# A decoder trunk's prologue: small tables loaded as rows, tile 0's gain behind its transposes, the first weight unit in halves, fillers on TensorE

## The chip, the cores and the metric

The kernel runs on one core of a Trainium2 chip. The metric is the device time of one execution in microseconds, the median of several. A core has TensorE (PE: matmuls, and PEld: its weight loads), VectorE (DVE), ScalarE (ACT), GpSimd (POOL) and SyncE (SP, which here only issues DMAs); each works off its own queue strictly in order, and they meet through semaphores. Sixteen DMA engines move data for all queues. The granted clock is the share of TensorE's full speed that the chip's throttle allowed.

## The reference

Two layers of a decoder trunk act on x of 512 tokens by 1024 features. Each layer normalizes x by its root mean square and a gain g (`norm_g`), projects it with one matrix to 3488 columns, feeds four head groups with these (latent attention, a short convolution, a spatial gate, block-sparse attention), multiplies each by a SiLU gate, projects back and adds the result to x.

```
def rmsnorm(x, g):
    xf = x.astype(jnp.float32)
    y = xf * lax.rsqrt(jnp.mean(xf * xf, axis=-1, keepdims=True) + EPS)
    return (y * g).astype(x.dtype)
...
    h = rmsnorm(x, norm_g)
    p = h @ w_in
...
    ang = pos.astype(jnp.float32)[..., None] * inv
    cos = jnp.cos(ang)[:, :, None, :]
    sin = jnp.sin(ang)[:, :, None, :]
```

The change touches only the way into the first layer: the loads of `positions`, g and the first weights, the normalization of x and the first projection. What is computed stays the same.

## The kernel before, in words

**Precision.** Every product is made of three matmuls (`mm3`, line 250). Both operands are split into a high part, which the reduced format fp32r holds, and a low part, the difference; hi by hi, hi by lo and lo by hi are summed in PSUM. So each weight and each activation is split once: ACT (sometimes DVE) copies it to the high part, and DVE subtracts (`split2`, line 245, and `split_units`, line 331).

**Tiles.** The 512 tokens are four tiles of 128. For each tile `pre_norm` (line 544) takes the sum of squares (ACT, two halves), lets GpSimd add the two and raise to the power -1/2 (two small steps on `xss`), multiplies x by that scale and by g on DVE to h, transposes h by eight 128x128 PE transposes in two groups of four (`hT`), and splits the result into `hTh` and `hTl`.

**Weights.** They arrive in units of at most 128x1024 elements, loaded in a fixed order by SP's queue (`load_units`, line 316). The first four, c0 to c3, hold the 416 columns of the first projection (`cq`): 256 contraction rows each, that is two of the eight k-steps. So k-steps 0 and 1 need c0, 2 and 3 c1, and so on. For every token tile, `tok` (line 1169) runs eight k-steps of three matmuls 128x416, 24 in all. A unit is split in two halves; a half is one k-step.

**Order.** A planner in Python (`Order` and `Chain`, lines 63 to 189) writes the program. Each piece of work is a generator, with a clock for each engine and a modelled cost for each operation; the planner emits an operation when its inputs are due by the model, smaller priorities first. What it emits is then the fixed order of each engine's queue. `o.now` is the modelled time of TensorE. A DMA is modelled at 360 bytes per ns plus 2 us. `LOAD_HOOKS` starts the loads of x tiles after given weight units. If the model is wrong, the order stays, and engines wait.

**The prologue** (`start`, line 1275). DVE sets a tile of ones and a zeroed tile `gz`; PE warms up with three matmuls of ones. SP loads x tile 0 in two halves, then g into the first row of `gz`, then c0, x tile 1, c1, c2, c3, x tiles 2 and 3. PE spreads g over 128 partitions by multiplying `gz` with the ones (`ng`, two PSUM tiles, kept until the last tile's h). GpSimd's queue loads the positions as a 128x4 tile of single elements (line 395); GpSimd and DVE later make the rope tables from it (`rope_tables`, line 400, from modelled time 7000 ns, with the lowest priority, in the gaps).

**After it.** Tile by tile: `cq`, its low-rank chain (`ct`, transposes `cT`, `q`, `kv`), then the unit sequence sq, ga, kv, su and so on, with the attention heads in between, then the output projection `o`, whose operands for block-sparse attention are called `yD`. Layer 1 follows in the same way.

## Time and profile before

| | before |
|---|---|
| median of 3 executions | 508.97 us (508.83 to 509.05) |
| profiled execution, its own time | 508.65 us |
| its span, first to last instruction | 506.8 us |
| PE busy | 498.1 us |
| mean granted clock of TensorE | 0.996 |
| first matmul of the first projection | 11.08 us |
| first weight unit c0: issued, in use from | 2.65, 7.78 us |
| positions: issued, in use from | 2.21, 7.30 us |

Times in the profile count from the start of the span. A row of the timeline gives start, duration, engine, source line, operation, output and inputs, shape and count; in brackets stand the time that the engine had been idle before and what ended it. All operations that the planner emits have line 158 (PE's: 184), so rows are told apart by their tiles: `whi_c` and `wlo_c` are the high and low part of a c unit, `sq` the squares, `xss` the scale, `h` the normalized tile, `hT` its transpose. Matmul durations overlap, since matmuls are pipelined; the step from one start to the next is their price.

### The profile page before, as it was taken

The page shows a single profiled execution, that of the slowest core. Times are in us where ns is not written, and L with a number is a line of the kernel's source. Part 1 is how long each engine was busy: PE and PEld are TensorE (multiplying, and loading weights), DVE is VectorE, ACT ScalarE, POOL GpSimd, SP SyncE. Part 2 cuts the span into 40 slices and gives each one's busy share as a digit, 9 for nine tenths or more (in the row PEclk, how much of TensorE's full clock was granted, in tenths as well). Part 3 has the DMA queues.
Part 4 walks back from the last instruction along what each step waited for, and adds up shares of the span by engine and source line. Part 5 has one row for each costly group of instructions (what it writes and reads, how often), then busy time and mean ns, then how long its engine had stood idle before and what let it go on. Part 6 is the DMA issues. An engine that isn't in the chain of part 4 may idle for free.

```text
span 506.8 us, 7665 instructions
## 1 busy us (share of the span) xinstructions
PE 498.1 (98%) x2508; PEld 423.3 (84%) x2508; DVE 349.3 (69%) x917; ACT 296.5 (58%) x891; POOL 139.2 (27%) x321
## 2 busy tenths in 40 slices
PE   6999999999999999999999999999999999999997
PEld 4898888888888888888889988888888888888886
DVE  4877975468799887635576988777868887635311
ACT  5698764567687775424247894677766777432100
POOL 6867875452000000000121488513330000000000
PEclk9999999999999999999999999999999999999999
DMA  8533415112114123464443242140142121624111
GB/s 273 165 123 114 125 43 166 41 43 66 60 43 166 52 74 109 142 175 117 143 155 126 83 125 71 55 124 2 42 167 82 43 83 49 201 84 164 66 54 50
DMA packets 20618, 51.57 MB, mean 102 GB/s; under 512 B 5985, under 2 KB 7265, under 8 KB 20578
## 3 DMA queue, kind: packets, MB, share of 16 engines
q1 hardware_dynamic: 20546, 51.08, 31.1%
q8 instruction: 20, 0.33, 0.3%
q0 software_dynamic: 32, 0.00, 0.1%
q14 instruction: 20, 0.16, 0.1%
HBM read 46.87 MB, written 4.19 MB: 101 GB/s over the span
## 4 chain that ended last, share of the span: by engine, by line
PE 90%; POOL 4%; DVE 2%; DMA 2%; ACT 1%; issue 1%; POOLq 0%; DVEq 0%
PE o L184 17%; PE kv L184 10%; PE cq L184 6%; PE sq L184 5%; PE cc L184 4%; PE gb L184 4%; PE cb L184 4%; PE gd L184 4%; PE gc L184 4%; PE ch L184 4%; PE su L184 4%; PE sa L184 3%; PE ga L184 3%; PE oa L184 2%; PE od L184 2%; PE sd L184 2%
## 5 line engine op out<-in xcount | busy, mean ns | idle before, releaser
L158 DVE TENSOR_TENSOR xr<-o,xr 128x512 f32<-128x512 f32 (+1 forms) x17 | 11.2, 658 | 42.0 <-PE o L184 42.0
L184 PE MATMUL o<-whi_wo,yTl 128*128 128x512 f32 (+1 forms) x102 | 38.4, 377 | 0.0
L184 PE MATMUL o<-wlo_wo,yTh 128*128 128x512 f32 (+1 forms) x102 | 38.4, 377 | 0.0
L184 PE MATMUL o<-whi_wo,yTh 128*128 128x512 f32 (+1 forms) x102 | 38.4, 376 | 0.0
L158 ACT ACTIVATE whi_wo<-raw_wo 128x512 fp32r<-128x512 f32 x31 | 18.3, 624 | 21.7 <-PE o L184 13.6
L158 ACT ACTIVATE pa<-pa,mna 128x256 f32<-128x256 f32 (+3 forms) x44 | 23.4, 539 | 5.2 <-DVE mna L158 5.1
L184 PE MATMUL kv<-whi_kv,hTh 128*128 128x512 f32 x64 | 26.0, 406 | 0.0
L184 PE MATMUL o<-whi_wo,yD 128*128 128x512 f32 (+1 forms) x68 | 25.7, 381 | 0.0
L158 ACT ACTIVATE pd<-pd,mnd 128x256 f32<-128x256 f32 (+3 forms) x46 | 24.5, 546 | 2.0 <-DVE mnd L158 1.5
L158 ACT ACTIVATE pha<-pTa 128x512 fp32r<-128x512 f32 (+3 forms) x32 | 13.9, 434 | 20.1 <-PE pTa L184 19.9
L184 PE MATMUL kv<-whi_kv,hTl 128*128 128x512 f32 x64 | 25.1, 392 | 0.0
L184 PE MATMUL kv<-wlo_kv,hTh 128*128 128x512 f32 x64 | 24.9, 390 | 0.0
L158 ACT ACTIVATE phd<-pTd 128x512 fp32r<-128x512 f32 (+3 forms) x32 | 13.9, 435 | 18.4 <-PE pTd L184 18.3
L184 PE MATMUL cq<-whi_c,hTh 128*128 128x416 f32 x64 | 24.3, 380 | 0.0
L184 PE MATMUL cq<-whi_c,hTl 128*128 128x416 f32 x64 | 23.3, 365 | 0.0
L184 PE MATMUL cq<-wlo_c,hTh 128*128 128x416 f32 x64 | 23.0, 360 | 0.0
L158 DVE TENSOR_TENSOR wlo_wo<-raw_wo,whi_wo 128x512 fp32r<-128x512 f32 x32 | 21.0, 687 | 2.4 <-ACT whi_wo L158 2.0
L184 PEld LDWEIGHTS o<-wlo_wo,yTh 128*128 128x128 f32 x102 | 19.2, 188 | 3.6
L184 PEld LDWEIGHTS o<-whi_wo,yTh 128*128 128x128 f32 x102 | 19.2, 188 | 3.6
L184 PEld LDWEIGHTS o<-whi_wo,yTl 128*128 128x128 f32 x102 | 19.2, 188 | 3.5
L158 DVE CUSTOM_DVE_ANT_0 pa<-sa,maskb 128x512 f32<-128x512 f32 (+3 forms) x32 | 15.0, 485 | 8.7 <-PE pTa L184 4.6
L158 DVE TENSOR_TENSOR pld<-pTd,phd 128x512 fp32r<-128x512 f32 (+3 forms) x32 | 15.5, 486 | 4.9 <-ACT phd L158 4.8
(328 smaller groups left out, 1712.8 us busy)
## 6 DMA issues: line engine op xcount, KB each, us to landing
raw_wo<-in_w_o_dram SPq DMA_DIRECT2D x16, 512.0 KB, 3.9
raw_sq<-in_w_t_dram SPq DMA_DIRECT2D x8, 512.0 KB, 3.5
raw_kv<-in_w_t_dram SPq DMA_DIRECT2D x8, 512.0 KB, 3.5
raw_c<-in_w_c_dram SPq DMA_DIRECT2D x8, 416.0 KB, 4.2
raw_ga<-in_w_f_dram SPq DMA_DIRECT2D x4, 512.0 KB, 3.6
raw_su<-in_w_f_dram SPq DMA_DIRECT2D x4, 512.0 KB, 3.5
raw_gc<-in_w_f_dram SPq DMA_DIRECT2D x4, 512.0 KB, 3.6
raw_ch<-in_w_f_dram SPq DMA_DIRECT2D x4, 512.0 KB, 3.4
```

What stands on the lines that cost most here:

```text
L158: f(*a, **k)
L184: f(*a, **k)
```

## The change

- The positions come as four rows of 128 by ACT's queue into `junk`; GpSimd casts them, one PE transpose turns them into a 128x4 tile, DVE copies it out (`posf`). g comes as eight rows of 128 by ACT's queue, and a PE transpose and a DVE copy make `gT`, 128x8, the gain of each feature by partition. The `gz` tile, its memset, its load and the `ng` matmuls are gone.
- Tile 0's h is x times the scale alone. Its gain is applied behind the transposes: ACT's copy to the high part scales by `gT`, and DVE multiplies and subtracts in one operation for the low part, both in pieces of one k-step (128 columns) in place of four. A tile's `hT` now has one event for each k-step. Tiles 1 to 3 multiply by g as before, from a 128x1024 copy that is now loaded by SP's queue behind c3 (`load_norm_gain`, as in layer 1).
- c0 is loaded in two halves. ACT makes both high parts. Both low parts are made by GpSimd, behind tile 0's scale (`split_first`). GpSimd also makes the low part of c1's second half and of c2's first half (`POOLLO`). Token tile 0 waits for a unit's half in place of the whole unit.
- The squares of tile 0 and 1 are shared between DVE (its first 640 or 512 columns, in one reducing operation) and ACT (the rest). x tile 0 is loaded in parts of 640 and 384 columns, and x tile 1 behind c1 in place of c0.
- Warm-up: two matmuls of ones ahead of the two small transposes, three behind. Until the planner's time 16000 ns, wherever PE waits by the model, transposes of the identity are put into 60% of the gap (`FILL`).
- Later starts and priorities: rope tables from 14000 ns in place of 7000, the mixing chain from 21000 in place of 23000, layer 0's parameters due at 16500 in place of 17500.

The lines that the diff removes from `pre_norm` and from the squares in `start` are printed above and left out here.

```
@@ -32,9 +32,11 @@
...
 AHEAD = 4
-NWARM, NWARM2 = 3, 1
-ROPET, MIXT = 7000.0, 23000.0
+NWARM, NWARM2, X0CUT = 2, 3, (640, 512)
+ROPET, MIXT = 14000.0, 21000.0
...
+FILL, FILLEND = 0.6, 16000.0
+POOLLO = (('c1_0', 1), ('c2_0', 0))
...
@@ -179,7 +181,11 @@
...
                 yield self.t + PEMARGIN
+        if self.o.now < self.o.fill_until:
+            for _ in range(int((self.o.now - self.o.pe_end) * FILL / 110.0)):
+                self.o.fill()
...
+        self.o.pe_end = self.o.now
...
@@ -322,7 +329,15 @@
...
                 u.raw = yield from rawS.get(ch, u.name)
-            dma(ch, P * u.a * u.b * 4, u.raw[:, :u.a * u.b], u.src)
+            n = u.a * u.b
+            if u.name == "c0_0":
+                for i in range(2):
+                    ch = Chain(o)
+                    sl = slice(i * n // 2, (i + 1) * n // 2)
+                    dma(ch, P * n * 2, u.raw[:, sl], u.src[:, sl])
+                    o.set(u.landed[i], ch.t)
+            else:
+                dma(ch, P * n * 4, u.raw[:, :n], u.src)
...
@@ -331,9 +346,13 @@
     def split_units():
...
             ch = Chain(o)
-            yield from ch.wait(u.loaded)
+            if u.name != "c0_0":
+                yield from ch.wait(u.loaded)
...
             n = u.a * u.b
+            if u.name == "c0_0":
+                yield from split_first(u, ch)
+                continue
...
@@ -346,16 +365,35 @@
...
                     yield from c2.act(A.activation, hi, raw, AF.Copy)
-                yield from c2.dve(V.tensor_tensor, lo, raw, hi.bitcast(F32), op=ALU.subtract)
+                if (u.name, i) in POOLLO:
+                    yield from c2.pool(G.tensor_tensor, lo, raw, hi.bitcast(F32), op=ALU.subtract)
+                else:
+                    yield from c2.dve(V.tensor_tensor, lo, raw, hi.bitcast(F32), op=ALU.subtract)
+                o.set(u.half[i], c2.t)
...
-    def unit(ch, name):
+    def split_first(u, ch):
+        n = u.a * u.b // 2
+        parts = [(u.hi[:, i * n:(i + 1) * n], u.lo[:, i * n:(i + 1) * n], u.raw[:, i * n:(i + 1) * n])
+                 for i in range(2)]
+        for i, (hi, _, raw) in enumerate(parts):
+            yield from ch.wait(u.landed[i])
+            yield from ch.act(A.activation, hi, raw, AF.Copy)
+        yield from ch.wait(layers[0].r0_ev)
+        for i, (hi, lo, raw) in enumerate(parts):
+            yield from ch.pool(G.tensor_tensor, lo, raw, hi.bitcast(F32), op=ALU.subtract)
+            o.set(u.half[i], ch.t)
+        u.raw_slots.put(ch)
+        o.set(u.ready, ch.t)
+    def unit(ch, name, half=None):
...
             v.wanted = True
-        yield from ch.wait(u.ready)
+        yield from ch.wait(u.ready if half is None else u.half[half])
...
@@ -389,10 +428,10 @@
...
     junk = cst.tile([P, GW], F32, name="junk")
-    posi = cst.tile([P, NT], I32, name="posi")
...
     inv = cst.tile([P, 16], F32, name="inv")
-    nc.gpsimd.dma_start(posi, dram(positions, 0, [[1, P], [P, NT]]))
+    nc.scalar.dma_start(junk[0:NT, 0:P].bitcast(I32), dram(positions, 0, [[P, NT], [1, P]]))
+    G.tensor_copy(junk[0:NT, P:2 * P], junk[0:NT, 0:P].bitcast(I32))
...
@@ -542,37 +580,61 @@
...
     def pre_norm(L, t, xx, t0, release):
...
+        late = L.l == t == 0
+        def half(c, t1):
+            c2 = Chain(o, t1)
...
             hput(c2)
...
+            nk = 1 if late else 4
+            todo = []
+            for k in range(0, 4, nk):
+                kt = c * 4 + k
+                hi, lo = (z[:, kt:kt + nk, t * P:(t + 1) * P] for z in (hTh, hTl))
+                src = tp[:, k * P:(k + nk) * P].rearrange("p (k n) -> p k n", k=nk)
+                ca = Chain(o, c2.t)
+                yield from ca.act(A.activation, hi, src, AF.Copy, **(dict(scale=gT[:, kt:kt + 1]) if late else {}))
+                todo.append((ca.t, kt, hi, lo, src))
+            for ta, kt, hi, lo, src in todo:
+                cv = Chain(o, ta)
+                if late:
+                    yield from cv.dve(V.scalar_tensor_tensor, lo, in0=src, scalar=gT[:, kt:kt + 1],
+                                      in1=hi.bitcast(F32), op0=ALU.mult, op1=ALU.subtract)
+                else:
+                    yield from cv.dve(V.tensor_tensor, lo, src, hi.bitcast(F32), op=ALU.subtract)
+                for i in range(nk):
+                    o.set(L.hT[t][kt + i], cv.t)
+            if c == min(t, 1):
+                o.set(L.hi_ev[t], ca.t)
+            trS.put(cv)
+        ch = Chain(o, t0)
+        s1 = L.xss[t]
+        eps = 0.0 if L.l == 0 and t < 2 else EPS
+        yield from ch.pool(G.tensor_scalar, s1[:, 2:3], s1[:, 0:1], s1[:, 1:2], eps, op0=ALU.add, op1=ALU.add)
+        yield from pow_rstd(ch, s1[:, 3:4], s1[:, 2:3], 1)
+        if t == 0:
+            o.set(L.r0_ev, ch.t)
+        if not late:
+            yield from ch.wait(L.ng_ev)
+        h = yield from hS.get(ch, f"h{t}_{L.l}")
+        hput = shared(hS, 2)
...
+            sl = slice(c * 512, (c + 1) * 512)
+            if late:
+                yield from ch.dve_fast(V.tensor_scalar, h[:, sl], xx[:, sl], s1[:, 3:4], None, op0=ALU.mult)
+            else:
+                yield from ch.dve(V.scalar_tensor_tensor, h[:, sl], in0=xx[:, sl], scalar=s1[:, 3:4], in1=L.ng[c],
+                                  op0=ALU.mult, op1=ALU.mult)
+            o.spawn(half(c, ch.t), None, t - NT)
+        release(ch)
+        if t == NT - 1:
+            for _ in range(2):
+                t2S.put(ch)
...
     def rope(ch, x1, x2, cb, sb, nh, nd, name):
...
@@ -1169,10 +1231,10 @@
         def tok(L, n, width, t, dst, us):
...
             for k in range(KT):
-                if n == "c" and k % 4 == 0:
-                    yield from m.wait(L.hT[t][k // 4])
-                if t == 0 and k % 2 == 0:
-                    us.append((yield from unit(m, f"{n}{k // 2}_{L.l}")))
+                if n == "c":
+                    yield from m.wait(L.hT[t][k])
+                if t == 0:
+                    us[k // 2:] = [(yield from unit(m, f"{n}{k // 2}_{L.l}", k % 2))]
...
@@ -1273,24 +1335,34 @@
...
     def start():
+        o.clk["D"] = 800.0
...
         ones = (yield from zzS.get(cw, "ones"))
-        gz = yield from hS.get(cw, "gz")
+        gn = ones[0:KT, 256:384]
+        nc.scalar.dma_start(gn, dram(norm_g, 0, [[P, KT], [1, P]]))
...
-        yield from cw.dve_fast(V.memset, gz, 0.0)
...
-        for _ in range(NWARM):
-            PE.matmul(wp[:, 0:256], ones[:, 0:P], ones[:, 0:256], start=True, stop=True)
+        def warm(n):
+            for _ in range(n):
+                PE.matmul(wp[:, 0:256], ones[:, 0:P], ones[:, 0:256], start=True, stop=True)
+        warm(NWARM)
+        PE.transpose(wp[:, 256:256 + NT], junk[0:NT, P:2 * P], ident[0:NT, 0:NT])
+        V.tensor_copy(posf, wp[:, 256:256 + NT])
+        PE.transpose(wp[:, 384:384 + KT], gn, ident[0:KT, 0:KT])
+        V.tensor_copy(gT, wp[:, 384:384 + KT])
+        warm(NWARM2)
+        o.pe_end, o.fill_until = 6300.0, FILLEND
+        o.fill = lambda: PE.transpose(wp[:, 0:P], ident, ident)
+        zzS.put(Chain(o, 6000.0))
+        accS.put(Chain(o, FILLEND + 200.0))
...
-        L0.ng = []
-        for c in range(2):
-            L0.ng.append((yield from sS.get(cg, f"ng{c}")))
...
         L0.x[0] = x0
-        for c in range(2):
-            dma(cg, P * 2048, x0[:, c * 512:(c + 1) * 512], x[0, 0:P, c * 512:(c + 1) * 512])
-            o.set(L0.x0[c], cg.t)
-        nc.sync.dma_start(gz[0:1, :], dram(norm_g, 0, [[D, 1], [1, D]]))
+        for c, sl in enumerate((slice(0, X0CUT[0]), slice(X0CUT[0], D))):
+            cx = Chain(o)
+            dma(cx, P * 4 * (sl.stop - sl.start), x0[:, sl], x[0, 0:P, sl])
+            o.set(L0.x0[c], cx.t)
...
         def after(t):
             def f():
@@ -1298,10 +1370,10 @@
...
             units[n].wanted = True
-        LOAD_HOOKS["c0_0"] = (after(1),)
-        LOAD_HOOKS["c3_0"] = (after(2), after(3))
+        LOAD_HOOKS["c1_0"] = (after(1),)
+        LOAD_HOOKS["c3_0"] = (lambda: o.spawn(load_norm_gain(L0)), after(2), after(3))
...
-        L0.par_t = 17500.0
+        L0.par_t = 16500.0
...
@@ -1309,25 +1381,28 @@
...
             def pre(t):
                 ch = Chain(o)
...
+                sq = yield from sS.get(ch, f"sq{t}")
+                if t:
+                    yield from ch.wait(L0.hi_ev[min(t - 1, 1)])
+                if t < 2:
+                    xt, s1, cut = L0.x[t], L0.xss[t], X0CUT[t]
+                    yield from ch.wait(L0.x0[0] if t == 0 else L0.xr[t])
+                    jk = yield from hS.get(ch, f"sqj{t}")
+                    yield from ch.dve(V.tensor_tensor_reduce, out=jk[:, 0:cut], in0=xt[:, 0:cut], in1=xt[:, 0:cut],
+                                      scale=1.0 / D, scalar=EPS, op0=ALU.mult, op1=ALU.add, accum_out=s1[:, 0:1])
+                    hS.put(ch)
+                    t1 = ch.t
+                    ch = Chain(o, L0.x0[1].t if t == 0 else max(L0.hi_ev[0].t, L0.xr[t].t))
+                    yield from ch.act(A.activation, sq[:, 0:D - cut], xt[:, cut:D], AF.Square, scale=D ** -0.5,
+                                      accum_out=s1[:, 1:2])
+                    ch.t = max(ch.t, t1)
+                else:
+                    yield from ch.wait(L0.xr[t])
+                    for c in range(2):
+                        yield from square_half(ch, L0, t, c, sq, L0.x[t])
...
                 yield from pre_norm(L0, t, L0.x[t], ch.t, v4S.put)
...
+            o.spawn(pre(t), None, t - NT)
...
```

51 lines of the change are left out of this document (6 added, 45 removed).

## The prediction

> **What bounds the kernel now.** I read the page first: one engine fills the span.
>
> ```profile
> PE 498.1 (98%) x2508; PEld 423.3 (84%) x2508; DVE 349.3 (69%) x917; ACT 296.5 (58%) x891; POOL 139.2 (27%) x321
> ```
>
> TensorE is busy for 98%, so only its idle or slow stretches can be won. The windows view places them (length, busy us of PE, PEld, DVE, ACT, POOL, granted clock, DMA share, GB/s).
>
> ```profile
> 4.74:8.15 3.41, 2.22 (x6) 0.86 (x5) 0.37 (x1) 0.56 (x3) 1.63 (x5) 1.00 0.92 226
> 8.15:11.56 3.41, 1.55 (x10) 1.11 (x10) 3.38 (x8) 2.26 (x7) 3.05 (x7) 1.00 1.04 422
> 11.56:14.98 3.42, 3.42 (x11) 3.15 (x11) 2.94 (x6) 3.15 (x8) 3.01 (x6) 0.50 1.02 402
> 14.98:22.26 7.28, 6.68 (x42) 6.01 (x40) 5.56 (x11) 4.28 (x13) 6.16 (x14) 1.00 0.33 99
> 22.26:503.30 481.04, 480.99 (x2440) 409.96 (x2437) 335.43 (x892) 283.69 (x860) 122.32 (x266) 1.00 0.30 96
> ```
>
> From 22.26 to the last matmul PE is idle for 0.05 us. Ahead of it lie an idle start, 3.42 us at half the clock, and a few holes. The timeline of PE gives the steps:
>
> ```profile
> 10.67 0.66 PE L184 MATMUL hT<-ident,h 128*128 128x128 f32 x4 [0.50 <-DVE h L158]
> 11.08 0.43 PE L184 MATMUL cq<-whi_c,hTh 128*128 128x416 f32 x1
> 12.10 0.55 PE L184 MATMUL cq<-whi_c,hTh 128*128 128x416 f32 x1
> 14.87 0.41 PE L184 MATMUL cq<-whi_c,hTl 128*128 128x416 f32 x1
> 17.83 0.60 PE L184 MATMUL hT<-ident,h 128*128 128x128 f32 x4
> 18.18 0.43 PE L184 MATMUL cq<-whi_c,hTh 128*128 128x416 f32 x1
> 18.64 0.35 PE L184 MATMUL cq<-whi_c,hTl 128*128 128x416 f32 x1
> 20.34 0.35 PE L184 MATMUL cq<-whi_c,hTl 128*128 128x416 f32 x1
> 21.25 0.55 PE L184 MATMUL cT<-ident,ct 128*128 128x128 f32 x3 [0.55 <-DVE ct L158]
> 22.26 0.43 PE L184 MATMUL cq<-whi_c,hTh 128*128 128x416 f32 x1
> ```
>
> Nine steps lie between 18.64 and 20.34: a cq matmul costs 0.189 us. Eight lie between 12.10 and 14.87: 0.346 us at the low clock. Tile 0's 24 cq matmuls run from 11.08, and at 18.18 tile 1 begins, with tile 0 and both transpose groups of tile 1 done. I call that **state S**; the sum is the time at which the new kernel reaches S. A transpose group costs 0.35 us (17.83 to 18.18). From 18.18 to 22.26 stand 12 matmuls (2.27), one such group and three cT transposes (at most 0.35 each): 2.97 us in 4.08, so 1.1 us more is lost after S.
>
> Why so late a start? Four rows of DVE and ACT, then SyncE and GpSimd:
>
> ```profile
> 3.45 0.60 ACT L158 ACTIVATE sq<-x 128x512 f32<-128x512 f32 x1 [1.37 <-DMA x<-in_x_dram]
> 7.78 0.39 DVE L158 CAST whi_c<-raw_c 128x416 fp32r<-128x416 f32 x1 [5.50 <-DMA raw_c<-in_w_c_dram]
> 8.71 0.74 DVE L158 SCALAR_TENSOR_TENSOR h<-x,xss,ng 128x512 f32<-128x512 f32 x1
> 13.05 0.58 DVE L158 TENSOR_TENSOR wlo_c<-raw_c,whi_c 128x416 fp32r<-128x416 f32 x1
> ```
>
> ```profile
> 2.21 0.99 POOL L395 DMA_DIRECT2D posi<-in_positions_dram  x1
> 2.30 0.30 SPq L1293 DMA_DIRECT2D gz<-in_norm_g_dram  x1
> 2.65 0.35 SPq L259 DMA_DIRECT2D raw_c<-in_w_c_dram  x1
> 5.04 0.30 POOL L158 TENSOR_SCALAR xss<-xss 128x1 f32<-128x1 f32 x1 [1.21 <-ACT sq L158]
> 5.42 0.58 POOL L158 TENSOR_TENSOR xss<-xss,nhalf 128x1 f32<-128x1 f32 x1
> 7.30 0.19 POOL L158 CAST posf<-posi 128x4 f32<-128x4 int32 x1 [1.30 <-DMA posi<-in_positions_dram]
> 11.64 0.99 POOL L158 TENSOR_SCALAR xss<-xss 128x1 f32<-128x1 f32 x1
> 13.04 1.04 POOL L158 TENSOR_TENSOR xss<-xss,nhalf 128x1 f32<-128x1 f32 x1
> ```
>
> Tile 0's scale is ready at 5.42 + 0.58 = 6.00, but DVE is stuck in its queue behind the first weight half, which lands at 7.78; h starts at 8.71. That load was issued at 2.65, behind gz. The DMA view from 5 to 6 us shows what held it:
>
> ```profile
> DMA packets 50, 0.08 MB, mean 82 GB/s; under 512 B 27, under 2 KB 27, under 8 KB 50
> ## 3 DMA queue, kind: packets, MB, share of 16 engines
> q1 hardware_dynamic: 33, 0.08, 68.4%
> q0 software_dynamic: 17, 0.00, 50.9%
> ```
>
> Queue q0 is the positions, element by element: half of the 16 engines' time for no bytes, 82 GB/s against 422 later.
>
> **The change part by part.** *Positions and g as rows.* 6 KB in two issues on ACT, 0.35 us each by SyncE's row at 2.65, before its first square at 3.45: hidden. The chain that they head is new: GpSimd waits for the positions before its cast (behind it 0.6 us of memsets and tile 0's scale), PE for cast and rows (behind it the warm-ups and the transposes), DVE for PE (behind it tile 0's square). The slow q0 packets go, and gz with its memset and its place before c0; so c0's two halves are issued at about 1.7 and 2.1 and land at about 4.7 and 5.3 (estimate: the 0.52 MB of x ahead of them, then 0.43 MB at 422 GB/s is 1.0 us). What is late next is not c0.
>
> *Tile 0's squares.* DVE's two-operand reduction, at two widths:
>
> ```profile
> L158 DVE CUSTOM_DVE_ANT_0 pa<-sa,maskb 128x512 f32<-128x512 f32 x8 | 5.5, 686 | 3.1 <-PE sa L184 3.0
> L158 DVE CUSTOM_DVE_ANT_0 pa<-sa,maskb 128x384 f32<-128x384 f32 x8 | 4.4, 554 | 1.6 <-PE pTa L184 1.6
> ```
>
> 640 columns: 0.686 + 0.132 = 0.82 us, from about 4.1 (x at 3.45 plus the wider part; the two small copies of posf and gT stand ahead of it on DVE and wait for PE, which waits for the rows). It ends near 5.0, where GpSimd began before (5.04). So the scale is again ready at 6.0; I book nothing. h follows at once, PE transposes at 6.5, the eight hi and eight lo pieces follow one by one (128 columns are 0.29 us by the same step, so four pieces cost DVE 0.5 us more than one of 512; beside PE's wait below), and the first cq matmul starts near 7.8 instead of 11.08. This early start is not the sum: weights come next.
>
> *Low parts on GpSimd.* Both halves of c0, c1's second and c2's first go to GpSimd, in a queue that begins when the scale is ready (6.0), and by the planner's own costs tile 1's two scale steps stand ahead of the fourth. k-steps 4 to 7 of tile 0 cannot start before that fourth part. The trace has no GpSimd subtraction 416 wide; its nearest rows:
>
> ```profile
> L158 POOL TENSOR_TENSOR mq<-mq,cosT x14: 244/252/285, 93.6 to 327.8; 128x32 f32<-128x32 f32 x14
> L158 POOL TENSOR_TENSOR Q<-Q,cosT x6: 313/320/862, 73.0 to 92.1; 128x64 f32<-128x64 f32 x6
> ```
>
> 32 more columns cost 0.068 us, so 416 cost 0.320 + 352 x 0.00213 = 1.07 us. The other end: the step at 13.04 took 1.04 against 0.58 at 5.42 and ended 0.45 after DVE's wlo_c of 13.05 to 13.63, as if it waited for it; one such wait of 0.58 makes 1.65. I take 1.3, between them, for the four, and 0.65 and 0.8 for tile 1's steps (0.30 to 0.99, 0.58 to 1.04). With 0.35 for the wait for c1's high part: 4 x 1.3 + 1.45 + 0.35 = 7.0, so 13.0. K-steps 5 to 7 then need three low parts of DVE at 0.58, one for each 0.57 us of PE: no further wait if DVE is free.
>
> The Trainium skill, "SBUF — State Buffer", section "SBUF: two separate sides", says that DVE with two SBUF inputs and a GpSimd instruction hold one port pair exclusively for a whole instruction. The row at 13.04 agrees; by that rule DVE's low parts and h would wait as well, and the sum would lie at the long end.
>
> *Then S.* Twelve matmuls 2.27, two transpose groups 0.70: 13.0 + 2.97 = 16.0, against 18.18: **2.2 us**. Of the 1.1 us lost after S I take 0.8 as won (ng no longer holds two PSUM slots; tile 2 has its x in time). Sum **3.0 us**.
>
> *The rest.* ng for tiles 1 to 3 becomes 0.52 MB of loads: 1.2 us at 422 GB/s; it lands near 11 (3.3 MB from 2.0 on), before tile 1's scale at about 11.7: hidden, and 1.2 us if GpSimd were quicker. Fillers stand only in gaps that the planner sees, 60% of each, about a dozen of 0.1 us, mostly ahead of k-step 4, where PE waits: nothing, at most 1.2 us. Warm-up moves inside idle time.
>
> Profile and times: 508.65 in the profiled execution, 1.85 over its span of 506.8; median 508.97. The sum of 3.0 leaves 503.8 of span, 505.65, and with the 0.32 between execution and median **506.0**.
>
> **The rivals.** *Free GpSimd.* With 1.07, 0.30 and 0.58: 6.0 + 5.5 = 11.5, S at 14.5, 3.7 + 1.1 = 4.8: 504.2. For it: 5.04 and 5.42 ran undisturbed. Against: DVE is busy 3.38 of 3.41 us at 8.15.
>
> *The clock falls again.* At 11.56 it fell after a window of which PE was busy for 1.55 of 3.41; at 8.15 it held after 2.22. In the new kernel PE waits before k-step 4 and lies between. If the window to 14.98 is slow again, the work from 13.0 does 0.99 in 1.98 us, S comes 1.0 later: 507.0. The fillers speak against it, if they count.
>
> The Trainium skill, "TensorE: Matmul & The Clock Gate", Part 4, says that transposes do not count as PE-busy in the same way. By that rule fillers would not hold the clock: this rival. The trace allows it, since the window ahead of 11.56 held eight transposes and only this of cq, but does not need it:
>
> ```profile
> 8.15:11.56 3.41, 0.48 (x2) 0.30 (x2) 0.00 (x0) 0.00 (x0) 1.00 1.04 422
> ```
>
> *Rows as late as elements.* If the small loads on ACT take what posi took (2.21 to 7.30, 5 us from an issue at 0.8), DVE's queue stands until about 6.3 behind the two copies, the scale comes at 8.1, everything 2.1 later: 508.1, no change that can be told. The x rows (issued 0.8, in at 3.45) speak against it.
>
> *Slower.* The rope tables start 7 us later (14 for 7) and behind GpSimd's new work. Attention waits for them, the output stage for attention:
>
> ```profile
> 72.13 0.25 POOL L158 TENSOR_SCALAR cosT<-rope_scratch 128x64 f32<-128x64 f32 x1
> L158 DVE TENSOR_TENSOR yD<-yad,yD x2: 681/683/685, 187.2 to 205.6; 128x512 fp32r<-128x512 f32 x2
> 227.14 0.39 PE L184 MATMUL o<-whi_wo,yD 128*128 128x512 f32 x1
> ```
>
> The last yD is done at 206.3 and first read at 227.14: 20.8 us in hand. The tables late by 7 plus four low parts (5.2) and PE early by 3 use 15. Beyond 20.8 each us costs one; from 24 the kernel is slower; at 27 it is 512.
>
> **How the numbers follow.** Forecast 506.0 with 0.48 (its own range 505.0 to 506.9); free GpSimd 0.22; clock 0.14; rows late 0.09; rope 0.07. The long end of GpSimd is 4 x 1.65 + 0.99 + 1.04 + 0.35 = 9.0: S at 17.95, 0.2 + 0.8 won, 508.0. Low 504.0 takes in the free case; high 507.7 nearly the long end, leaving out rows late and rope. A measurement of this kernel tells about 0.2%, 1.0 us, from no change: 507.95 to 509.99. Faster: 0.48 + 0.22 + 0.14 = 0.84; same 0.09; slower 0.07.
>
> **What would show it.** Right: c0 landed by 5.5, first cq near 7.8, GpSimd's four wlo_c at 1.3 each, k-step 4 near 13.0, S near 16, PE without idle from there. Wrong: PE waiting for ng's DMA at S, a granted clock of 0.50 after 8, wlo_c under 1.1 or over 1.6, or PE idle near 225.

## The result and the profile after

The changed kernel takes **509.73 us** (median, 509.11 to 510.18), the kernel before 508.86 on the same chip (508.42 to 509.83): ratio 1.0018, 95% interval 1.0011 to 1.0026. It is slower by 0.9 us; 506.0 was forecast. Its profiled execution took 509.11, with a span of 507.4, against 508.65 and 506.8.

From the page, PE's line; then the windows view of the changed kernel, cut at its own steps (columns as in the prediction: length, busy us of PE, PEld, DVE, ACT, POOL, granted clock, DMA share, GB/s), and the one window of the kernel before that is needed beside it.

```profile
PE 498.8 (98%) x2523; PEld 423.5 (83%) x2523; DVE 351.7 (69%) x932; ACT 294.4 (58%) x889; POOL 139.9 (28%) x316
```

```profile
9.47:17.95 8.48, 7.57 (x48) 6.27 (x47) 8.20 (x20) 4.45 (x12) 4.79 (x6) 1.00 0.93 322
17.95:20.83 2.88, 2.88 (x18) 2.79 (x17) 2.19 (x7) 2.82 (x11) 0.50 (x2) 1.00 0.31 101
20.83:50.00 29.17, 28.45 (x152) 25.39 (x151) 25.22 (x75) 23.70 (x101) 22.82 (x40) 1.00 0.40 121
50.00:300.00 250.00, 249.89 (x1259) 212.90 (x1258) 176.99 (x472) 152.82 (x468) 68.90 (x155) 1.00 0.32 102
300.00:330.00 30.00, 29.18 (x141) 24.30 (x140) 24.62 (x78) 17.90 (x64) 19.97 (x41) 1.00 0.28 90
```

```profile
300.00:330.00 30.00, 29.95 (x148) 25.00 (x147) 24.30 (x81) 17.94 (x61) 20.74 (x47) 1.00 0.26 73
```

Two things are to be seen. While tile 0 is projected, DVE is the full engine (8.20 of 8.48 us), not GpSimd (4.79). And PE, idle for 0.05 us in all from 22.26 on in the kernel before, now idles 0.72 us between 20.83 and 50 and 0.82 between 300 and 330. PE's timeline has the steps:

```profile
7.52 0.66 PE L190 MATMUL hT<-ident,h 128*128 128x128 f32 x4 [0.29 <-DVE h L160]
...
9.47 0.44 PE L190 MATMUL cq<-whi_c,hTh 128*128 128x416 f32 x1
...
14.52 0.45 PE L190 MATMUL cq<-wlo_c,hTh 128*128 128x416 f32 x1 [0.90 <-POOL wlo_c L160]
...
17.95 0.35 PE L190 MATMUL cq<-whi_c,hTh 128*128 128x416 f32 x1
...
20.48 0.44 PE L190 MATMUL cq<-whi_c,hTh 128*128 128x416 f32 x1
...
24.72 0.48 PE L190 MATMUL kv<-whi_ukv,cTh 128*128 128x512 f32 x1
25.92 0.50 PE L190 MATMUL kv<-wlo_ukv,cTh 128*128 128x512 f32 x1 [0.72 <-DVE wlo_ukv L160]
...
317.53 0.28 PE L190 MATMUL mp<-vnh,wsh 128*128 128x256 f32 x1
318.63 0.39 PE L190 MATMUL mp<-vnl,wsh 128*128 128x256 f32 x1 [0.82 <-DVE vnl L160]
...
503.74 0.28 PE L190 MATMUL o<-whi_wo,yD 128*128 128x256 f32 x1
```

And of the kernel before, at the later of the two waits and at its last matmul:

```profile
317.38 0.28 PE L184 MATMUL mp<-vnh,wsh 128*128 128x256 f32 x1
317.71 0.38 PE L184 MATMUL mp<-vnl,wsh 128*128 128x256 f32 x1
...
503.05 0.28 PE L184 MATMUL o<-whi_wo,yD 128*128 128x256 f32 x1
```

**The account.** State S (tile 1's first cq matmul) comes at 17.95, only 0.23 earlier than 18.18; 16.0 was forecast. At 20.48 four k-steps of tile 1 and three cT are done; the kernel before had the same and one more transpose group (0.35) behind it at 22.26. So the lead is 22.26 - 20.83 = 1.4 us: the 0.2, the 1.1 lost after S, all of it won, and 0.1 that the cT took less than the 0.35 booked for them. Then it is given back: from 24.72 to 25.92 a step of 0.23 takes 1.20 (0.97 lost), at 74 us 0.26 is lost, and from 317.53 to 318.63 a step of 0.12 takes 1.10 (0.98 lost, 0.21 at that place before). 1.4 - 0.97 - 0.26 - 0.77 = -0.6; the last matmul starts at 503.74 against 503.05.

The start, in the timelines of DVE, GpSimd and ACT:

```profile
5.31 0.55 ACT L160 ACTIVATE whi_c<-raw_c 128x416 fp32r<-128x416 f32 x1 [0.34 <-DMA raw_c<-in_w_c_dram]
5.57 0.58 POOL L160 TENSOR_TENSOR xss<-xss,nhalf 128x1 f32<-128x1 f32 x1
6.12 2.27 POOL L160 TENSOR_TENSOR wlo_c<-raw_c,whi_c 128x416 fp32r<-128x416 f32 x2
6.19 2.49 DVE L160 TENSOR_SCALAR h<-x,xss 128x512 f32<-128x512 f32 x2 [1.20 <-POOL xss L160]
9.40 0.35 DVE L160 SCALAR_TENSOR_TENSOR hTl<-hT,gT,hTh 128x128 fp32r<-128x128 f32 x1 [0.44 <-ACT hTh L160]
10.16 0.37 DVE L160 CAST whi_c<-raw_c 128x416 fp32r<-128x416 f32 x1
10.62 1.09 POOL L160 TENSOR_TENSOR wlo_c<-raw_c,whi_c 128x416 fp32r<-128x416 f32 x1 [2.22 <-DVE whi_c L160]
12.44 0.30 POOL L160 TENSOR_SCALAR xss<-xss 128x1 f32<-128x1 f32 x1 [0.73 <-DVE xss L160]
12.83 0.58 POOL L160 TENSOR_TENSOR xss<-xss,nhalf 128x1 f32<-128x1 f32 x1
12.97 1.94 DVE L160 TENSOR_TENSOR wlo_c<-raw_c,whi_c 128x416 fp32r<-128x416 f32 x2
13.37 1.09 POOL L160 TENSOR_TENSOR wlo_c<-raw_c,whi_c 128x416 fp32r<-128x416 f32 x1
14.84 0.76 DVE L160 SCALAR_TENSOR_TENSOR h<-x,xss,ng 128x512 f32<-128x512 f32 x1
```

The scale (`xss`) is ready at 6.15 and c0's high part starts at 5.31, as forecast. But tile 0's two h take 2.49 us beside GpSimd's two low parts. GpSimd then waits 2.22 us for a cast that stands in DVE's queue behind a low piece of hT and a low part, and 0.73 for DVE's square of tile 1; the fourth low part ends at 14.46. Tile 1's scale is ready at 13.41, but its h starts at 14.84, behind two DVE low parts that took 0.97 each beside GpSimd's.

### The profile page after: what moved, and what is told of

Its sections match the earlier page's. It is cut to its first block, busy times and chain, and to the rows that moved or that the text cites. A ratio compares the mean times of both kernels' runs of the same rounds, so it can differ in the third digit from the quotient of the medians.

```text
span 507.4 us, 7709 instructions
## 1 busy us (share of the span) xinstructions
PE 498.8 (98%) x2523; PEld 423.5 (83%) x2523; DVE 351.7 (69%) x932; ACT 294.4 (58%) x889; POOL 139.9 (28%) x316
## 4 chain that ended last, share of the span: by engine, by line
PE 85%; POOL 5%; ACT 5%; DVE 4%; issue 1%; POOLq 0%; ACTq 0%
PE o L190 17%; PE kv L190 10%; PE cq L190 6%; PE gb L190 4%; PE cb L190 4%; PE cc L190 4%; PE ch L190 4%; PE gd L190 4%; PE gc L190 4%; PE su L190 4%; PE sa L190 3%; ACT junk L160 2%; PE sd L190 2%; PE od L190 2%; PE oa L190 2%; PE pTa L190 2%
## 5 line engine op out<-in xcount | busy, mean ns | idle before, releaser
L160 ACT ACTIVATE pha<-pTa 128x512 fp32r<-128x512 f32 (+3 forms) x32 | 13.8, 438 | 19.7 <-PE pTa L190 19.2
L160 DVE TENSOR_TENSOR wlo_wo<-raw_wo,whi_wo 128x512 fp32r<-128x512 f32 x32 | 21.1, 686 | 4.4 <-ACT whi_wo L160 4.2
L160 ACT ACTIVATE phd<-pTd 128x512 fp32r<-128x512 f32 (+3 forms) x32 | 13.9, 436 | 15.4 <-PE pTd L190 15.2
L190 PEld LDWEIGHTS o<-whi_wo,yTh 128*128 128x128 f32 x102 | 19.2, 188 | 3.5
L190 PEld LDWEIGHTS o<-wlo_wo,yTh 128*128 128x128 f32 x102 | 19.2, 188 | 3.5
L190 PEld LDWEIGHTS o<-whi_wo,yTl 128*128 128x128 f32 x102 | 19.2, 188 | 3.5
L160 DVE TENSOR_TENSOR pla<-pTa,pha 128x512 fp32r<-128x512 f32 (+3 forms) x32 | 15.1, 486 | 9.2 <-ACT pha L160 9.1
```

Source lines behind the costliest of these rows:

```text
L160: f(*a, **k)
L190: f(*a, **k)
```

## The experiments

Three questions: what holds the start (is it that DVE's and GpSimd's instructions exclude each other, called the lock below, or GpSimd's queue order, or DVE's load), where the later waits come from, and what the fillers are worth. Every ratio is against the kernel before on the same chip.

**Rows alone.** The kernel before, with only the positions loaded as rows.

```
-    nc.gpsimd.dma_start(posi, dram(positions, 0, [[1, P], [P, NT]]))
+    nc.scalar.dma_start(junk[0:NT, 0:P].bitcast(I32), dram(positions, 0, [[P, NT], [1, P]]))
...
+        PE.transpose(wp[:, 256:256 + NT], junk[0:NT, P:2 * P], ident[0:NT, 0:NT])
```

> The kernel before, with one part of the change alone: positions as four rows by ACT's queue, GpSimd's cast, one small PE transpose, DVE's copy. Theory A (the element-wise load of the positions held the DMA engines from 5 to 7 us): no q0 packets, c0 is in use from 5.5 to 6.2 in place of 7.78, h at about 6.9 in place of 8.71, first cq near 9.3 in place of 11.08; total 1.0 to 1.8 us less than before, 507.2 to 508.0. Theory B (c0 was late for its own packets): c0 still at 7.3 to 7.8, total as before, 508.9.

508.66 us, ratio 0.9991 (0.9982 to 1.0000). DVE's and PE's timeline:

```profile
6.27 0.38 DVE L158 CAST whi_c<-raw_c 128x416 fp32r<-128x416 f32 x1 [1.70 <-DMA raw_c<-in_w_c_dram]
8.88 0.75 DVE L158 SCALAR_TENSOR_TENSOR h<-x,xss,ng 128x512 f32<-128x512 f32 x1 [0.34 <-PE ng L184]
10.98 0.46 PE L184 MATMUL cq<-whi_c,hTh 128*128 128x416 f32 x1 [0.25 <-ACT hTh L158]
```

The reading of queue q0 was right: without it c0 is in use at 6.27 instead of 7.78. The 1.0 to 1.8 us of theory A did not follow, because the second h then waits for PE's ng, and the first cq matmul comes at 10.98 (11.08).

**h on ACT.** Tile 0's h leaves DVE.

```
-                yield from ch.dve_fast(V.tensor_scalar, h[:, sl], xx[:, sl], s1[:, 3:4], None, op0=ALU.mult)
+                yield from ch.act(A.activation, h[:, sl], xx[:, sl], AF.Copy, scale=s1[:, 3:4])
```

> The changed kernel, with the two operations of tile 0's h on ACT (a copy with the scale by partition) in place of DVE. Theory A (shared port): ACT shares nothing with GpSimd, so h takes 0.6 to 0.7 us each from about 6.9 (behind c0's second high part), GpSimd's low parts stay at 1.1 each and start at 6.1, second transposes near 8.3, first cq near 8.3, S near 17.2. Theory B (h is slow for what it reads, x just loaded): 1.2 us each on ACT too, second transposes at 9.3, S near 18.2. Total: A about 509.0, B about 510, if the later waits stay.

508.99 us, ratio 1.0001 (0.9991 to 1.0010), S at 17.54. The time is theory A's; its first cq matmul (8.3) is not, that comes at 9.41, while k-step 4's second matmul comes at 13.91 instead of 14.52. ACT makes the two h in 1.32 us, not slowed. What DVE then does beside GpSimd's low parts is slowed in their place (timeline of GpSimd and DVE): a cast that takes 0.36 to 0.39 elsewhere takes 1.24.

```profile
6.39 2.10 POOL L160 TENSOR_TENSOR wlo_c<-raw_c,whi_c 128x416 fp32r<-128x416 f32 x2
7.49 1.24 DVE L160 CAST whi_c<-raw_c 128x416 fp32r<-128x416 f32 x1 [2.21 <-DMA raw_c<-in_w_c_dram]
```

**Low parts planned behind h.** A miss: it only moved the event by which the planner orders.

```
-        if t == 0:
-            o.set(L.r0_ev, ch.t)
...
+        if t == 0:
+            o.set(L.r0_ev, ch.t)
         release(ch)
```

> The changed kernel, with GpSimd's two low parts of c0 allowed only behind both operations of tile 0's h, in place of behind its scale. In the changed kernel the two h operations of DVE took 2.49 us beside GpSimd's 2.27 us of low parts. Theory A (they exclude each other at the shared port): alone the two take 0.9 to 1.0 us, the second transposes of tile 0 start near 7.3 in place of 8.73, the first cq near 8.2 in place of 9.47, and the low parts run from about 7.1 to 9.4. State S (tile 1's first cq) moves from 17.95 to about 17.0, since c1's parts follow sooner on DVE. Theory B (this form of h costs 1.2 us by itself): h still takes about 2.5 us, everything behind it is 1.1 to 2.3 us later, S near 19. The total follows S only as far as the waits behind it stay as they are (kv 0.97, mp 0.25 and 0.98 us in the changed kernel): A 508.8, B 510.8.

509.48 us, ratio 1.0011 (1.0002 to 1.0020). No data ties GpSimd's low parts to h, so they still started at 6.11, beside it, and the two h took 2.50. It tells nothing apart.

**Low parts behind h by data.** One GpSimd copy of a column of h ahead of them; every other instruction keeps its place.

```
-            o.set(L.r0_ev, ch.t)
+        tr = ch.t
...
+        if late:
+            G.tensor_copy(s1[:, 2:3], h[:, D - 1:D])
+            o.set(L.r0_ev, tr)
```

> The changed kernel with one GpSimd instruction more: a copy of one column of h's second half ahead of the two low parts of c0, so that these start by data behind both h; every other instruction stands in the same order. Theory A (GpSimd's subtractions hold DVE's h through the shared SBUF ports): the two h take 0.9 us together instead of 2.49 and end near 7.1, the first transposes of h follow the warm-ups at 7.3, the second group near 7.9, the first cq matmul comes at 8.4 to 8.9 instead of 9.47, c1's second high part on DVE near 9.4 instead of 10.16, k-step 4's low part ready 0.5 to 0.8 earlier, S near 17.3. The time is 0.4 to 0.8 below the changed kernel if nothing gives it back. Rival B (1.24 us is what this h costs, whatever GpSimd does): two h again 2.4 to 2.5, first cq 9.4 to 9.6, S 17.9, same time.

509.12 us, ratio 1.0005 (0.9996 to 1.0014). Timeline:

```profile
6.28 0.88 DVE L160 TENSOR_SCALAR h<-x,xss 128x512 f32<-128x512 f32 x2 [1.19 <-POOL xss L160]
8.79 0.44 PE L190 MATMUL cq<-whi_c,hTh 128*128 128x416 f32 x1
9.01 0.77 DVE L160 CAST whi_c<-raw_c 128x416 fp32r<-128x416 f32 x1 [1.85 <-DMA raw_c<-in_w_c_dram]
14.80 0.46 PE L190 MATMUL cq<-wlo_c,hTh 128*128 128x416 f32 x1 [0.89 <-POOL wlo_c L160]
```

Theory A holds for the lock: the two h take 0.88 instead of 2.49, and the first cq matmul comes 0.68 earlier. In this profile the gain stops there: DVE waits for c1's data until 9.01, k-step 4's second matmul comes at 14.80, S at 18.23. But c1's data came later here than in any other profile of these loads in which DVE waits for it (7.49 with h on ACT), and the profiled execution, 509.47, is one of the two longest of the eleven. The median is 0.6 us below the changed kernel, as theory A had it, and the run with h on ACT is 0.7 below. So the lock is real; what it costs in the time is perhaps these 0.6 us (the intervals of the ratios touch), and S in one profile doesn't show it.

**No low parts of c1 and c2 on GpSimd** (`POOLLO = ()`).

> The changed kernel, with the low parts of c1's second and c2's first half on DVE again (GpSimd keeps c0's two). In the changed kernel k-step 4 waited 0.9 us for GpSimd's c2 part at 14.46, which stood behind tile 1's two scale steps. Theory A (GpSimd's queue is the limit): k-step 4 starts at 13.2 to 13.6 in place of 14.52, S near 17.0. Theory B (DVE, with its one-k-step pieces, is the limit and GpSimd only waits for it): DVE has 1.2 us more, tile 1's square and h come later, S at 18.0 to 19.0. Total: A about 508.9, B 510 or more, if the later waits stay.

514.25 us, ratio 1.0100 (1.0076 to 1.0124). It is theory B: k-step 4's second matmul starts at 14.52 again, although no low part of GpSimd's stands ahead of it, and S comes at 17.84. Then DVE falls behind: PE's cT waits for it, and the profiled execution is at half clock from 31.0 to 34.4.

```profile
29.99 0.55 PE L190 MATMUL cT<-ident,ct 128*128 128x128 f32 x3 [2.65 <-DVE ms L160]
```

**GpSimd's order.** Tile 1's scale steps behind c2's low part.

```
+        if L.l == 0 and t == 1:
+            yield from ch.wait(units["c2_0"].half[0])
```

> The changed kernel with one wait in its plan: tile 1's two scale steps on GpSimd stand behind c2's low part instead of ahead of it. In the changed kernel GpSimd idles 2.22 us before c1's low part (it waits for DVE's high part) and 0.73 us before tile 1's scale (it waits for DVE's square), and c2's low part, which k-step 4 waits for, stands behind. Theory G (that queue order sets k-step 4): c2's low part runs from 11.7 to 12.8, k-step 4's second matmul starts at 12.8 to 13.2 instead of 14.52, S at 16.3 to 17.0, and the time is 0.5 to 1.5 us below the changed kernel unless a later wait eats it. Rival T (DVE's low parts of c2 and c3 and tile 1's h come no earlier): k-step 4 earlier, but k-steps 5 to 7 or tile 1's transposes wait instead, S 17.6 to 18.2, same time.

511.01 us, ratio 1.0048 (1.0034 to 1.0061). Timeline:

```profile
13.52 0.45 PE L190 MATMUL cq<-wlo_c,hTh 128*128 128x416 f32 x1
...
18.41 0.56 DVE L160 TENSOR_TENSOR ct<-cq,cg_b 128x384 f32<-128x384 f32 x1 [1.28 <-DMA cg_b<-in_mla_kv_norm_g_dram]
...
18.89 1.28 DVE L160 TENSOR_TENSOR hTl<-hT,hTh 128x512 fp32r<-128x512 f32 x2
...
19.62 0.55 PE L190 MATMUL cT<-ident,ct 128*128 128x128 f32 x3 [2.00 <-DVE hTl L160]
```

K-step 4 runs a microsecond earlier, and tile 0's last cq matmul starts at 15.53. So theory G holds for that step. The time is lost behind it: tile 1's first cq matmul comes only at 19.93. The planner now puts cT ahead of tile 1's matmuls and, on DVE, ct ahead of tile 1's low pieces. The two PSUM slots for transposes (`trS`) are held by tile 1's hT until DVE has made hTl; hTl stands behind ct, and ct waits for a parameter that lands at 18.4. The profiled execution, 512.94, is the longest of five, with half clock from 21.1 to 24.5; the other four, 510.88 to 511.62, had a mean clock of 1.000.

**c3's low parts off DVE.** They are replaced by a scaled copy on ACT, so this kernel leaves out c3's low part. Here the plan of layer 1, the second layer, is that of the kernel before already (the edit of the run after next).

```
+                if u.name == "c3_0":
+                    yield from c2._emit("V", 68 + 1.047 * (n // 2), A.activation, (lo, raw, AF.Copy), dict(scale=2.0 ** -12))
```

> The same second layer's plan, with c3's two low parts replaced by a scaled copy of c3 on ACT (the output is not the reference's): two of DVE's three low parts that stand ahead of tile 1's h are gone, every other instruction keeps its place, ACT is idle there. Theory V (DVE's queue from 9.4 to 16.7 us is a second limit beside GpSimd's: tile 1's h waits for it, its scale being ready 1.4 us before): the first h starts 0.6 to 1.0 us earlier after the scale (within 0.6 us of it instead of 1.4), the second one 1.0 to 1.6 us earlier, both transpose groups of tile 1 follow without a wait, and tile 1's first cq matmul comes 0.3 to 0.6 us earlier counted from k-step 4's low part, no more, because k-step 4 still waits for GpSimd; the time is 0.2 to 0.6 us below 508.9. Rival W (only GpSimd's low part of c2 counts): tile 1's first cq matmul keeps its distance of 3.4 us from k-step 4's low matmul, and the time stays within 0.15 us.

508.84 us, ratio 1.0000 (0.9991 to 1.0009), against 508.91 with them. Tile 1's first h starts 0.06 us after its scale instead of 1.43, as theory V says, though it now runs beside GpSimd's low part (the two h take 2.25 us instead of 0.76 and 0.74). Tile 1's first cq matmul comes at 18.54 in both profiles. These can't tell V from W: in both PE works at half speed until about 13 us and has no wait of 0.2 us from its first cq matmul to that place. The median can, and it is rival W's: taking this load from DVE is not worth anything by itself.

**Starts back** (`ROPET, MIXT = 7000.0, 23000.0`).

> The changed kernel with the starts of the rope tables and of the mixing weights as before (7000 and 23000 in place of 14000 and 21000). The lead of 1.4 us that the changed kernel has near 21 us is gone at the end. Theory P (these two starts put DVE work into 17 to 26 us, and with it the waits of 0.97 us for wlo_ukv at 24.72 and of 0.98 us for vnl at 317.53): both waits fall under 0.3 us and the time is 1.0 to 1.7 below the changed kernel, 508.0 to 508.7, below the kernel before. Rival Q (the waits come from the early part itself, whose plan any change of costs shifts): one or both stay within 0.2 us of what they were, or others of that size stand in their place; time 509.3 to 510.

509.73 us, ratio 1.0014 (1.0005 to 1.0023). Theory P falls: 0.93 us are lost at 25.08 and 0.96 at 318.22, as without the edit.

**Layer 1's plan.** Two side effects of the change taken back outside the prologue.

```
-                    us[k // 2:] = [(yield from unit(m, f"{n}{k // 2}_{L.l}", k % 2))]
+                    us[k // 2:] = [(yield from unit(m, f"{n}{k // 2}_{L.l}", k % 2 if n == "c" and l == 0 else None))]
...
-            o.spawn(half(c, ch.t), None, t - NT)
+            o.spawn(half(c, ch.t), None, t - NT if L.l == 0 else 0)
```

> The changed kernel with two side effects of the change taken out of everything but the first layer's start: only the first layer's c units are waited for by halves, and the transposes of h run ahead of other work in the first layer alone. With that the second layer's instructions stand on every engine in the order of the kernel before; the first 40 us keep the changed kernel's order on PE but for what the two edits move there. Theory L (these side effects re-planned the second layer, and that re-planning is where the second part of the lead went): the wait of 0.98 us for vnl near 317 us falls to the 0.2 us of the kernel before, the waits at 9 to 25 us stay, and the time is 0.6 to 0.9 us below the changed kernel, 508.8 to 509.1. Rival M (the wait belongs to the moment at which the second layer starts or to the tables): it stays over 0.7 us and the time with it.

508.91 us, ratio 0.9997 (0.9988 to 1.0006): 0.8 us won back, as theory L says. The last half of every engine's instruction list is then that of the kernel before, and PE is full again around 317 (windows view):

```profile
300.00:330.00 30.00, 29.94 (x145) 24.92 (x144) 24.27 (x82) 18.48 (x63) 20.91 (x47) 1.00 0.23 71
```

In the changed kernel the low part vnl stood in DVE's queue behind a step (mq) that waited for GpSimd (timeline of the changed kernel):

```profile
316.29 1.13 POOL L160 TENSOR_TENSOR mmq<-mmq,nhalf 128x4 f32<-128x4 f32 x1
317.45 0.34 DVE L160 SCALAR_TENSOR_TENSOR mq<-mq,mmq,dq_b 128x64 f32<-128x64 f32 x1 [0.71 <-POOL mmq L160]
318.15 0.42 DVE L160 TENSOR_TENSOR vnl<-vn,vnh 128x256 fp32r<-128x256 f32 x1
```

The 0.26 us lost at 74 us have the same form: mq waits 0.94 us for GpSimd's mmq, and vnl stands behind it until 73.56.

**Tile 3's squares later** (on top of that).

```
-                    yield from ch.wait(L0.hi_ev[min(t - 1, 1)])
+                    yield from ch.wait(L0.hi_ev[t - 1])
```

> The same, and tile 3's squares wait for tile 2's high pieces instead of tile 1's, so that DVE's four h instructions of tiles 2 and 3 do not stand together ahead of the second wlo_ukv. Theory D (the wait of 0.97 us at 24.7 us is DVE's queue: h of tile 3 ahead of wlo_ukv): the wait falls under 0.3 us, no other over 0.5 us stands in its place before 40 us, and the time is another 0.6 to 1.0 us lower, 507.9 to 508.4. Rival E (DVE has too much to do between 20 and 27 us in any order): a wait of 0.5 to 1.0 us stands at another place between 18 and 35 us, and the time is that of the run above.

513.24 us, ratio 1.0081 (1.0067 to 1.0095). Theory D's first part came, the rest did not: the wait at 25 us shrinks to 0.25, and a larger one than either theory had comes at 37.88, where cT waits for a low piece of hT, now late, on DVE.

```profile
37.88 0.55 PE L190 MATMUL cT<-ident,ct 128*128 128x128 f32 x3 [2.80 <-DVE hTl L160]
```

**ukv ahead of tile 3's h** (on layer 1's plan).

```
+        if L.l == 0 and t == 3:
+            yield from ch.wait(units["ukv_0"].ready)
```

> The changed kernel with the second layer's plan as before, and in the first layer tile 3's h behind ukv's parts in DVE's queue (one h fewer ahead of the second wlo_ukv). Theory D (the wait of 0.97 us for wlo_ukv near 25 us is that queue, and nothing else is late there): the wait falls to 0.2 to 0.4 us, tile 3's start stays within 0.4 us, and the time is 0.5 to 0.8 us below the 508.9 of the second layer's plan alone: 508.1 to 508.4, just below the kernel before. Rival E (DVE is full between 22 and 35 us, any order makes something late): another wait of 0.5 us or more takes its place before 36 us, 508.7 to 509.2.

**508.01 us**, ratio 0.9982 (0.9974 to 0.9991): the first version below the kernel before. DVE around 25 us, of the changed kernel and then of this one, with PE's two matmuls:

```profile
24.00 1.41 DVE L160 SCALAR_TENSOR_TENSOR h<-x,xss,ng 128x512 f32<-128x512 f32 x2
25.33 0.54 DVE L160 TENSOR_TENSOR wlo_ukv<-raw_ukv,whi_ukv 128x256 fp32r<-128x256 f32 x1
```

```profile
25.50 0.47 PE L190 MATMUL kv<-whi_ukv,cTh 128*128 128x512 f32 x1
24.77 0.74 DVE L160 SCALAR_TENSOR_TENSOR h<-x,xss,ng 128x512 f32<-128x512 f32 x1
25.43 0.45 DVE L160 TENSOR_TENSOR wlo_ukv<-raw_ukv,whi_ukv 128x256 fp32r<-128x256 f32 x1
25.94 0.51 PE L190 MATMUL kv<-wlo_ukv,cTh 128*128 128x512 f32 x1
```

One h instead of two stands ahead of wlo_ukv; the wait falls from 0.97 to 0.21 (0.44 from 25.50 to 25.94, less the 0.23 of a step). Theory D holds: the wait was the order of DVE's queue. PE's order between 37 and 182 us differs too in this version; of the 0.86 us by which its profile beats that of layer 1's plan alone, 0.55 are there at 29 us.

**h on ACT and layer 1's plan together.** The edits of both.

> The same second layer's plan, and tile 0's h on ACT instead of DVE (which took 0.7 us off the changed kernel when it was done alone). If the two savings of 0.8 and 0.7 us are in different places, as their traces say (the second layer at 317 us; the first 18 us and the wait at 25 us), they add: 508.0 to 508.4, below the kernel before by 0.1 to 0.2%. If they overlap: 508.7 to 509.1.

509.54 us, ratio 1.0013 (1.0004 to 1.0022): they do not add, the two together are slower than each alone. The wait near 317 is gone, and others stand elsewhere, 0.49 us for a low piece of hT at 26.69 and one at 218:

```profile
218.45 0.33 PE L190 MATMUL pTd<-ident,pd 128*128 128x128 f32 x1 [0.42 <-DVE pld L160]
```

**All at once.** GpSimd's order, tile 3's squares, layer 1's plan, and c0's low parts on DVE.

> The three edits above together, and c0's two low parts on DVE behind its two h in place of GpSimd. If G, D and L hold and the lock at h is gone: two h 0.9 us, first cq 8.3 to 8.9, S 16 to 16.8, no wait over 0.4 us at 25 and 317 us, time 506.3 to 507.3, below both kernels. If only L and D hold: 507.9 to 508.5. If DVE's added 1.2 us are missed at 9 to 13 us: S 17.5 to 18, 508.0 to 508.8.

514.16 us, ratio 1.0097 (1.0083 to 1.0110), outside all three forecasts: PE idles as in the two runs that it contains, 2.29 us ahead of cT at 19.95 and 2.24 ahead of a transpose group at 39.35.

**No fillers** (`FILL = 0.0`), in the changed kernel, in it with the low parts behind h and the starts back, and in the version with ukv first.

> The changed kernel without the filler transposes (nothing else moves). Theory C (they only stand in the way): the granted clock stays at 1.00 from 8 us on, the first cq matmul starts 0.25 earlier, the second k-step another 0.25, but k-step 4 still waits for GpSimd's low part at 14.5, so S and the time stay within 0.3 us of the changed kernel. Rival H (they hold the clock): a window with a granted clock of 0.50 appears between 11 and 19 us, for 3.4 us, and the time is 1.0 us or more above the changed kernel.

> The three edits above together: c0's low parts on GpSimd wait for h, the two starts as before, no fillers. If A, P and C all hold: h 0.9 us, first cq 8.2 to 8.7, S near 17, no wait over 0.3 us at 25 and 317 us, span 505.2 to 506.0, time 507.0 to 507.8, below both kernels. If P falls: 508.7 to 509.5. If the clock falls without fillers: a window of 0.50 and 1.0 us on top.

> The kernel with ukv's parts first (508.01, ratio 0.9982), without the filler transposes; every other instruction keeps its place. In its profiled execution nine fillers ran for 0.9 us right ahead of k-step 4, when its low part was ready. Theory C (fillers cost where PE is late and nothing else): the time is 0.3 to 0.9 us lower, 507.1 to 507.7, ratio 0.9964 to 0.9976. Rival H (they bring the clock up or hold it often enough to pay for themselves): 508.0 to 508.9, ratio 0.998 to 1.000.

509.68 (1.0018, 1.0008 to 1.0028); 510.32 (1.0020, 1.0009 to 1.0031); 508.24 (0.9997, 0.9987 to 1.0007). In the medians nothing is won by leaving them out, so theory C's gain with ukv first did not come. The mean granted clock of the single executions shows why. With fillers it was 0.999 or 1.000 in all 12 executions of the changed kernel and all 11 with ukv first. Without them it was 0.997 or less in 2 of 11, 8 of 11 and 5 of 11. With ukv first those five took 508.93 to 509.29 us and the other six 507.58 to 508.24; with fillers all eleven took 507.65 to 508.40. So both theories hold in part: the fillers cost about 0.2 us where the clock holds, and without them it sometimes falls, for about 1.2 us. The profile of the second version shows such a stretch: PE idles 2.01 us ahead of k-step 4's second matmul, and half clock follows from 15.4 to 18.8. That version was not run with fillers, so its 510.32 is no price by itself.

## Why the prediction was wrong, step by step

- **Rows, halves of c0, scale at 6.0**: right (c0's high part at 5.31, scale at 6.15), and the reason was right, by the run with rows alone.
- **"h follows at once, PE transposes at 6.5", first cq near 7.8**: wrong, 7.52 and 9.47. It is no term of the sum. GpSimd's low parts were put into the very moment at which h starts and priced as if h ran beside them. The Trainium skill, "SBUF — State Buffer", section "SBUF: two separate sides", was cited for this; the measurements agree: 2.49 us beside them, 0.88 without. What that cost is open: the medians of the two runs that free h of it are 0.6 and 0.7 us below the changed kernel, but the profile of the first has S no earlier (18.23, with c1's data at 9.01).
- **GpSimd's 7.0 us from 6.0, k-step 4 at 13.0**: the first step of the sum that failed. The prices were too high (1.09 to 1.14 for a low part, 0.30 and 0.58 for the steps: 5.3 us of work in place of 6.65), but the queue was counted as continuous, with 0.35 of waiting; it waited 2.22 and 0.73 us for DVE. It ended at 14.46, and k-step 4's second matmul started at 14.52.
- **S at 16.0**: 17.95. That this is the number of the long end is luck: there GpSimd's pieces take 1.65 each and wait for nothing. That k-step 4 follows GpSimd's order is shown (13.52 in the run with that order); that S would follow k-step 4 is not: in that run the next waits stood right behind.
- **0.8 of the 1.1 us after S**: all 1.1 came.
- **"From 22.26 PE idles 0.05 us", read as PE without idle afterwards in the new kernel too**: the second step that failed, and it set the sign. No term of the sum stood for the planner writing a new order for everything behind. By the medians 0.8 us of what was given back is layer 1's new order (0.77 of it the wait at 317 us) and 0.9 what ukv ahead of tile 3's h won (0.76 of it the wait at 25 us): with both put right, the time is 508.01 and not 509.73. PE, without idle behind 22 us before, has no slack there for an order that the planner's model misjudges. The terms add up: S 1.95 us late, 0.3 more won behind it and 2.0 given back make 509.65 of the 506.0.
- **The rivals**: the clock did not fall in any of the 12 executions of the changed kernel, the rows were in time, the rope tables were no wait (PE does not wait near 225). Free GpSimd had the right prices and the wrong sum. The slower case was given to the tables; it came from the order.
- **Fillers at nothing**: right for the median of the changed kernel. But the clock fell in 7 of 22 executions of the changed kernel and of ukv first without them, and in none of 23 with them. So the runs speak against the rival that fillers would not hold the clock. The versions without them ran partly on other chips, but on the chip of the first two, two more versions with fillers (low parts behind h, starts back) kept 0.999 or more in all 22 executions.

Open: why S stays between 17.5 and 18.7 in most versions (19.2 to 20.3 in four). Three near limits were each seen when another was taken away: c1's data, in use from 7.49 to 9.01 in different runs; GpSimd's order with DVE's queue; the parameter at 18.4. A fourth is PE itself, where the first matmuls run at half speed until 13 us. No run took all away.

## What to carry to other kernels

When a planner writes the order, price an early gain only as far as the next place where order matters, and compare the queues of the untouched stages: here two edits meant for the prologue changed layer 1. Work moved to an idle engine is worth what its inputs allow: write down for each instruction of its queue when the other engine delivers, and what that engine holds back meanwhile. Take such a change apart by undoing its side effects one at a time, with every other instruction in its place.

## What the runs showed of the hardware

DVE instructions that read only SBUF took longer beside GpSimd's subtraction: h of tile 0 1.24 us each instead of 0.44, a cast 1.24 instead of 0.36, a low part 0.97 instead of 0.58, two h of tile 1 2.25 instead of 1.50. They look like waits for its end: that cast ended at 8.73, 0.24 us after GpSimd's second low part. DVE's low pieces of hT, which read PSUM, were not slowed: four in 1.12 us (0.28 each) from 10.45, beside GpSimd's low part of 10.62 to 11.71, and three in 0.86 from 12.19. ACT's two h beside two such low parts took 0.66 each, about ACT's 0.60 for 512 columns elsewhere.

The time at which the first matmuls run at full speed differs from run to run, from before 8 us to about 13.6; in layer 1's plan alone a cq matmul still takes 0.69 at 11.97 and 0.35 at 13.01, and that version was faster in the median than the changed kernel, whose profile was at full speed from 7.5 on. There PE had no wait ahead of k-step 4, where the changed kernel's had 0.90 us for a low part, and S came 0.59 us later: most of the late clock fell into time that PE would have waited.
